# Head norms sent through DRAM, prepared blocks copied apart, softmax scaled on ScalarE

## The chip, the cores and the metric

The kernel runs on one core of one Trainium2 chip. A core has five engines with a queue each: TensorE (PE in the profile; its weight loads are PEld), VectorE (DVE), ScalarE (ACT), GpSimd (POOL) and SyncE (SP). ScalarE and SyncE also issue DMAs; an instruction that waits at the head of a queue holds everything behind it. The metric is the device time of one execution in microseconds. The kernel before takes 897.43 us (median of three runs, 896.43 to 899.38).

## The reference

One encoder layer in fp32 over 512 tokens (two sequences of 256, d_model 1024), with three branches on the same normalised input, each gated and projected, summed and projected once more:

```python
proj = rmsnorm(x) @ w_in                      # 1024 -> 9952 columns
# A: gated delta rule, 8 heads of 128, both directions, chunks of 64
o_gdn = rmsnorm(o_fwd + o_bwd, gdn_norm_gain) * silu(z_gdn)
# B: low-rank attention with rotary keys, 8 heads
p = softmax(q_full @ k_full.T * scale);  o_mla = (p @ v_mla) * silu(z_mla)
# C: cross attention into 256 memory tokens, 4 heads
o_mem = (softmax(qx @ km.T * scale) @ vm) * silu(z_mem)
merged = g0 * (o_gdn @ w_br_gdn) + g1 * (o_mla @ w_br_mla) + g2 * (o_mem @ w_br_mem)
y = rmsnorm(x + merged @ w_out)
```

The norm of branch A is one number for each token and head: the root of the mean square over the head's 128 channels.

## The kernel before

All activations are kept with channels on the partitions and the 512 tokens along the row. Every product is done in three passes of rounded fp32 (high times high, low times high, high times low). A weight tile of 512 KB is therefore loaded by SP, rounded to its high part by ScalarE (`wh_`, line 205) and subtracted to its low part by VectorE or, for the qkv, qn and qm tiles, GpSimd (`wl_`, line 209). Each of the three has two buffers. One tile gives 24 products of 512 columns (`gemm`, line 237).

The work has three stages. `front` does the memory branch and the low-rank attention (branch B), with projection tiles from the list `fill` put between. `attend` does one softmax: scores on TensorE, the maximum on VectorE, the exponential with its sum on ScalarE (`p_a`, line 301), the reciprocal of the sum (line 304) and the scaling (line 306) on VectorE, and then transpositions on TensorE (`pt_a`). `middle` does the gated delta rule: `weave` runs several chains (preparation of two groups of four heads, loads, inputs, two solving lanes, outputs) against an estimated clock `self.now`, and each `yield` gives the time that TensorE spends and the time to wait; while no chain is due, it takes tiles from `fill`. The order on TensorE is that of the writing there; the other engines are ordered by a scheduler, in which a chain's number (1000 for the preparation, 300 for inputs, 2000 for lanes and outputs) is its rank. `back` does the last branch product and the output.

What the change touches in `middle`: `gdn_prep` inverts small triangular blocks on VectorE (lines 821 and 823, 31 rounds) and then copies them with seven activations into `t32` and `y32` (lines 843 to 848). `gdn_out` sums the squares of a head's output over the partitions (`so`, line 1086), raises them to -1/2 on GpSimd (`ro`, line 1089), copies each of the 512 numbers to all 128 partitions with four products against the unit matrix (`rob`, line 273), and multiplies the head's output `og` by them (line 1094), which VectorE reads from PSUM. Then `og` is split into the two rounded parts `xg` that the branch product of `back` (`gm_bg`) reads.

`mem_v` starts the kernel. Its first activation (line 215) brings a load of ScalarE's function table.

Of the kernel before, what the change touches and what calls it, by code (L numbers as in the profile page):

```python
# [13 lines left out]
P = 128  # L14
# [26 lines left out]
def _consts():  # L41
    t = np.arange(P)
    b = t // 32
    same = b[:, None] == b[None, :]
    le = t[:, None] <= t[None, :]
    ge = t[:, None] >= t[None, :]
    z, o = np.zeros((P, P)), np.ones((P, P))
    a8 = np.arange(8)
    anc = np.zeros((P, 2, 2, 8))
    for tb in range(2):  # L50
        tg = tb * P + t
        anc[:, 0, tb] = tg[:, None] >= 32 * a8[None]
        anc[:, 1, tb] = tg[:, None] < 32 * (a8[None] + 1)
    i32 = np.arange(32)
    m = (t % 32)[:, None]
    parts = [
        ("id", np.eye(P)), ("bd", same),
        ("anc", anc.reshape(P, 32)),
        ("trf", m <= i32), ("trb", m >= i32), ("i32", m == i32),
        ("ngf", np.where(i32 > m, 0.0, NEG)), ("ngb", np.where(i32 < m, 0.0, NEG)),  # L60
        ("one", np.ones((P, 1))), ("hf", np.full((P, 64), -0.5)), ("ph", np.full((P, 16), 0.5)),
    ]
# [92 lines left out]
class Layer:  # L155
# [39 lines left out]
    def weight(self, src, n, name, pool=None):  # L195
# [13 lines left out]
        eng.tensor_tensor(lo[:, :n], raw[:, :n], hi[:, :n].bitcast(F32), op=ALU.subtract)  # L209
# [65 lines left out]


    def attend(self, h, s, score, scale, vs, op, name):
# [27 lines left out]
        for qb in range(2):  # L305
            nc.vector.tensor_scalar(pt[:, qb], pt[:, qb], rs[:, qb:qb + 1], None, ALU.mult)
# [423 lines left out]
    def gdn_prep(self, g):  # L730
# [109 lines left out]
        for a in range(4):  # L840
            r = slice(32 * a, 32 * a + 32)
            d = a % 2
            nc.scalar.activation(t32[r], (o2 if d else o1)[r, :, 16 * d:16 * d + 16].rearrange("p i u -> p u i"), AF.Copy)
            yield 0.0, 1.5
        nc.scalar.activation(y32[:, 0:16], o2[:, :, 0:16].rearrange("p i u -> p u i"), AF.Copy)
        yield 0.0, 2.5
        for q in range(2):
            nc.scalar.activation(y32[:, 16 + q:32:2], o1[:, :, 17 - q:32:2].rearrange("p i u -> p u i"), AF.Copy)
            yield 0.0, 1.5
        self.ready[g] = self.now + 10  # L850
# [202 lines left out]
    def gdn_out(self, hh):  # L1053
# [195 lines left out]
    def run(self):  # L1249
        nc = self.nc  # L1250
        with ExitStack() as st:
# [7 lines left out]
            self.d_xa = dp.tile([P, 8, 512], F32, name="d_xa")  # L1259
            self.d_m = dp.tile([8, P, 512], F32, name="d_m")  # L1260
# [19 lines left out]
    def plan(self):  # L1280
# [22 lines left out]
        self.fill += g[12:13] + z[4:5] + ze[2:3] + vt[6:7] + qv(7) + g[13:14] + z[5:6] + ze[3:4] + vt[7:8] + g[14:15] + xe  # L1303
        self.fill += z[6:7] + g[15:16] + z[7:8] + [(self.split_x, self.xe)]
# [68 lines left out]
    def middle(self):  # L1373
# [154 lines left out]
```

## Time and profile before

| | |
|---|---|
| median of three runs | 897.43 us (896.43 to 899.38) |
| profiled execution | 899.75 us, span 898.0 us, mean granted clock 0.993 |
| TensorE busy | 868.4 us (97%) |
| VectorE busy | 580.8 us (65%) |
| ScalarE busy | 458.0 us (51%) |
| GpSimd busy | 201.6 us (22%) |
| DMA | 114.03 MB, mean 127 GB/s |

Busy time on TensorE is time in which some product is under way; the granted clock is 1.00 at full speed. Idle time before an instruction is put down to what ended last before it. A shorter operation off TensorE changes the time only where TensorE waits for it.

### The profile page before, as it was taken

The numbers are of one execution on the slowest core, as the hardware profiler recorded it, in microseconds if no ns is written. First come the engines' busy times: TensorE is split into PE (matmuls) and PEld (weight loads), VectorE is DVE, ScalarE is ACT, GpSimd is POOL, SyncE is SP. The second block draws the span as 40 slices with busy tenths as digits, with TensorE's granted clock in tenths as the row PEclk, the third lists the DMA queues.
The fourth block names the chain that finished last, engine by engine and source line by source line (L and its number), as shares of the span: only waits on it lengthen the run. The fifth ranks groups of instructions, "written<-read, shape, count | busy, mean of one in ns | idle before, by whom it ended". The sixth has DMA issues, their size and how long they took to land.

```text
span 898.0 us, 13279 instructions
## 1 busy us (share of the span) xinstructions
PE 868.4 (97%) x4908; PEld 709.8 (79%) x4908; DVE 580.8 (65%) x993; ACT 458.0 (51%) x879; POOL 201.6 (22%) x149
## 2 busy tenths in 40 slices
PE   6999999999999989999999999999999999999996
PEld 5878886878888778877788877777888888888886
DVE  6685337876769999546689994757445444336643
ACT  6654455545544445466675658766563533213332
POOL 0230341121112210226133423422210001332221
PEclk9999999999999999999999999999999999999998
DMA  9312221442234322454323343444433436465332
GB/s 332 117 65 94 82 77 47 129 150 74 101 104 144 108 78 95 163 162 143 108 95 108 130 148 114 147 118 132 156 113 103 142 130 227 139 205 193 118 95 94
DMA packets 49313, 114.03 MB, mean 127 GB/s; under 512 B 6752, under 2 KB 12000, under 8 KB 49248
## 3 DMA queue, kind: packets, MB, share of 16 engines
q1 hardware_dynamic: 44496, 104.52, 35.6%
q10 hardware_dynamic: 4752, 8.65, 2.7%
q8 instruction: 39, 0.64, 0.3%
q14 instruction: 26, 0.21, 0.1%
HBM read 93.03 MB, written 16.97 MB: 123 GB/s over the span
## 4 chain that ended last, share of the span: by engine, by line
PE 79%; DVE 10%; ACT 4%; DMA 3%; issue 2%; POOL 1%; SPq 0%; ACTq 0%; POOLq 0%; DVEq 0%
PE gm_g L237 13%; PE gm_qkv L237 10%; PE gm_bm L237 5%; PE gm_z L237 5%; PE gm_bg L237 5%; PE y L1195 4%; PE gm_za L237 4%; PE vm L366 3%; PE gm_be L237 3%; PE gm_qm L237 3%; PE gm_km L237 3%; PE gm_cq L237 2%; PE s_a L287 2%; PE o L1070 2%; PE kk L920 2%
## 5 line engine op out<-in xcount | busy, mean ns | idle before, releaser
L209 POOL TENSOR_TENSOR wl_qkv<-wr_qkv,wh_qkv 128x1024 fp32r<-128x1024 f32 x24 | 59.8, 2493 | 138.5 <-ACT wh_qkv L205 53.3
L698 DVE SCALAR_TENSOR_TENSOR kq<-cz,prm,kq 128x510 f32<-128x510 f32 (+1 forms) x64 | 53.7, 838 | 20.6 <-ACT kq L691 20.1
L237 PE MATMUL gm_g<-hh,wh_g 128*128 128x512 f32 x192 | 53.7, 411 | 4.2 <-ACT cz L689 2.3
L209 DVE TENSOR_TENSOR wl_g<-wr_g,wh_g 128x1024 fp32r<-128x1024 f32 x24 | 29.8, 1242 | 38.5 <-ACT wh_g L205 15.0
L237 PE MATMUL gm_qkv<-hh,wh_qkv 128*128 128x512 f32 x192 | 51.7, 408 | 2.1 <-ACT gt_g L1129 1.2
L237 PE MATMUL gm_g<-hl,wh_g 128*128 128x512 f32 x192 | 52.0, 403 | 0.0
L237 PE MATMUL gm_g<-hh,wl_g 128*128 128x512 f32 x192 | 52.0, 401 | 0.0
L237 PE MATMUL gm_qkv<-hl,wh_qkv 128*128 128x512 f32 x192 | 51.9, 403 | 0.0
L237 PE MATMUL gm_qkv<-hh,wl_qkv 128*128 128x512 f32 x192 | 51.4, 400 | 0.0
L237 PEld LDWEIGHTS gm_g<-hh,wh_g 128*128 128x128 f32 x192 | 35.6, 192 | 13.0 <-ACT cz L689 3.2
L1165 POOL TENSOR_TENSOR mg<-mg,lg 128x512 f32<-128x512 f32 x16 | 28.2, 1760 | 74.5 <-DVE lg L1164 58.3
L237 PEld LDWEIGHTS gm_qkv<-hh,wh_qkv 128*128 128x128 f32 x192 | 35.8, 192 | 10.8 <-ACT gt_g L1129 1.6
L237 PEld LDWEIGHTS gm_qkv<-hl,wh_qkv 128*128 128x128 f32 x192 | 36.2, 191 | 8.7 <-issue 0.4
L237 PEld LDWEIGHTS gm_g<-hl,wh_g 128*128 128x128 f32 x192 | 36.0, 191 | 8.1
L237 PEld LDWEIGHTS gm_qkv<-hh,wl_qkv 128*128 128x128 f32 x192 | 35.2, 188 | 7.7
L237 PEld LDWEIGHTS gm_g<-hh,wl_g 128*128 128x128 f32 x192 | 35.2, 189 | 7.5
L1195 PE MATMUL y<-wh_wo,mh 128*128 128x512 f32 (+1 forms) x144 | 40.0, 370 | 0.0
L821 DVE TENSOR_TENSOR tm<-xx,tt 128x1 f32<-128x1 f32 (+30 forms) x62 | 38.5, 622 | 1.0
L205 ACT ACTIVATE wh_g<-wr_g 128x1024 fp32r<-128x1024 f32 x24 | 25.4, 1057 | 24.8 <-PE gm_g L237 10.8
L205 ACT ACTIVATE wh_qkv<-wr_qkv 128x1024 fp32r<-128x1024 f32 x24 | 25.4, 1057 | 24.3 <-DVE tm L821 5.2
L910 POOL TENSOR_TENSOR kl<-kq,kh 128x512 fp32r<-128x512 f32 x16 | 21.7, 1361 | 67.1 <-ACT kh L908 46.4
L237 PE MATMUL gm_bm<-xa,wh_bm 128*128 128x512 f32 x128 | 33.2, 399 | 0.0
(400 smaller groups left out, 2250.0 us busy)
## 6 DMA issues: line engine op xcount, KB each, us to landing
wr_qkv<-in_w_dram SPq DMA_DIRECT2D x24, 512.0 KB, 3.3
wr_g<-in_w_dram SPq DMA_DIRECT2D x24, 512.0 KB, 3.4
e<-d_r SPq DMA_DIRECT2D x64, 96.0 KB, 3.0
wr_z<-in_w_dram SPq DMA_DIRECT2D x12, 512.0 KB, 3.4
wr_za<-in_w_dram SPq DMA_DIRECT2D x8, 512.0 KB, 3.5
d_g<-gt_g ACTq DMA_DIRECT2D x16, 256.0 KB, 2.0
wr_bm<-in_w_dram SPq DMA_DIRECT2D x8, 512.0 KB, 3.3
lg<-d_g SPq DMA_DIRECT2D x16, 256.0 KB, 3.3
```

The source lines that it names most:

```text
L205: self.wround = nc.scalar.activation(hi[:, :n], raw[:, :n], AF.Copy).ins
L209: eng.tensor_tensor(lo[:, :n], raw[:, :n], hi[:, :n].bitcast(F32), op=ALU.subtract)
L237: nc.tensor.matmul(ps[:m], a[:, k * m:(k + 1) * m], xs[k][j], start=n == 0, stop=n == 3 * nk - 1)
L287: nc.tensor.matmul(sp[:, qb * 256:(qb + 1) * 256], a, b, start=j == 0, stop=j == n - 1)
L366: nc.tensor.matmul(vps[tb], ms[k][a][:, t], b[:, :512], start=k == 0 and i == 0, stop=k == 7 and i == 2)
L698: nc.vector.scalar_tensor_tensor(ys, zs, self.cw[:, f, m:m + 1], ys, ALU.mult, ALU.add)
L821: nc.vector.tensor_tensor(t3, xx[:, i:i + 1, 0:i].to_broadcast([P, i, i]), tt[:, 0:i, 0:i], op=ALU.mult)
L910: nc.gpsimd.tensor_tensor(lo, src, hi.bitcast(F32), op=ALU.subtract)
L920: nc.tensor.matmul(ps, a[:, k], b, start=i == 0, stop=i == 2)
L1070: nc.tensor.matmul(out, ub[:, d, s, cp], rhs, start=n == 0, stop=n == 3)
L1165: nc.gpsimd.tensor_tensor(self.merged[d], self.merged[d], gt, op=ALU.add)
L1195: nc.tensor.matmul(ps, xs[2 * j + q][a][:, t], b[:, q * 512 + c0:q * 512 + c1], start=j == 0 and n == 0, stop=j == 3 and n == 5)
```

## The change

Five things are edited. The head norms: `store_cols` transposes the column of norms to rows on VectorE and stores it in DRAM with four small DMAs on SP's queue; a chain of its own, `heads_norm`, comes at least 10 us later by the estimated clock, loads the row back to all partitions with one DMA on ScalarE's queue (`load_row`, behind the last weight rounding written so far), waits 6 us more, and multiplies and splits `og` in `gdn_norm`. The seven copies of the preparation each stand behind the last weight rounding, with longer steps between them, and the preparation's rank falls from 1000 to 100. The scaling of the softmax in branch B moves to ScalarE. A one-column activation is put at the start. Two small things: a constant is narrower, and the loads of `xe` stand one tile later in `fill`.

```diff
@@ weight
-        eng.tensor_tensor(lo[:, :n], raw[:, :n], hi[:, :n].bitcast(F32), op=ALU.subtract)
+        d = eng.tensor_tensor(lo[:, :n], raw[:, :n], hi[:, :n].bitcast(F32), op=ALU.subtract)
+        if eng is nc.vector:
+            self.wsplit = d.ins
@@ new
+    def store_cols(self, r, i):
+        nc = self.nc
+        nc.vector.transpose(out=self.rt, in_=r)
+        for b in range(4):
+            nc.sync.dma_start(self.d_n[i].rearrange("(j b i) -> b j i", j=4, b=4)[b], self.rt[32 * b:32 * b + 4])
+    def load_row(self, dst, i):
+        with self.tc.issue_after(self.wround):
+            self.nc.scalar.dma_start(dst, self.d_n[i:i + 1].to_broadcast([P, 512]))
@@ attend
-            nc.vector.tensor_scalar(pt[:, qb], pt[:, qb], rs[:, qb:qb + 1], None, ALU.mult)
+            if name[0] == "a":
+                nc.scalar.activation(pt[:, qb], pt[:, qb], AF.Copy, scale=rs[:, qb:qb + 1])
+            else:
+                nc.vector.tensor_scalar(pt[:, qb], pt[:, qb], rs[:, qb:qb + 1], None, ALU.mult)
@@ mem_v
+        warm = self.p0.tile([P, 1], F32, name="warm")
+        nc.vector.memset(warm, 0.0)
+        nc.scalar.activation(warm, warm, AF.Square)
@@ gdn_prep (the three kinds of copies alike)
-            nc.scalar.activation(t32[r], (o2 if d else o1)[r, ...].rearrange("p i u -> p u i"), AF.Copy)
-            yield 0.0, 1.5
+            with self.tc.issue_after(self.wround):
+                nc.scalar.activation(t32[r], (o2 if d else o1)[r, ...].rearrange("p i u -> p u i"), AF.Copy)
+            yield 0.0, 2.8
...
-        self.ready[g] = self.now + 10
+        self.ready[g] = self.now + 4
@@ gdn_out
-        rr = self.p0.tile([P, 4], F32, tag="c4", bufs=4, name=f"ro{hh}")
+        rr = self.rr[:, 0:4]
         nc.vector.tensor_scalar(rr, ssp[:, 0:4], 1.0 / 128, 128 * EPS * EPS, ALU.mult, ALU.add)
         nc.gpsimd.tensor_tensor(rr, rr, c("hf")[:, 0:4], op=ALU.pow)
-        yield 0.9, 7.0
-        bp = self.ps_ms(par, f"rob{hh}")
-        self.bcast(rr, bp)
+        self.store_cols(self.rr, hh)
+        self.og[hh] = og, self.now + 10.0
         yield 0.9, 0.0
-        nc.vector.tensor_tensor(og, og, bp, op=ALU.mult)
+
+    def gdn_norm(self, hh):
+        nc = self.nc
+        og = self.og[hh][0]
+        rb = self.tb(f"rob{hh}")
+        self.load_row(rb, hh)
+        yield 0.0, 6.0
+        with self.tc.issue_after(self.wsplit):
+            nc.vector.tensor_tensor(og, og, rb, op=ALU.mult)
         hl = self.pk.tile([P, 2, 512], F32R, tag="kq", bufs=8, name=f"xg{hh}")
         self.split(og, hl[:, 0], hl[:, 1], 0.5)
@@ plan, middle
-  ... + g[14:15] + xe + z[6:7] + g[15:16] + ...
+  ... + g[14:15] + z[6:7] + xe + g[15:16] + ...
-            self.weave((self.preps(), 1000), ..., (self.heads_out(), 2000))
+            self.weave((self.preps(), 100), ..., (self.heads_out(), 2000), (self.heads_norm(), 1500))
+    def heads_norm(self):
+        for h in range(8):
+            while h not in self.og or self.now < self.og[h][1]:
+                yield 0.0, 1.0
+            yield from self.gdn_norm(h)
```

The first place is ScalarE's queue in the attention stage, at one softmax of head 6 (`p_a61`), before the change (`wh_` is a weight's rounding, `gt_` a gate, `ph_` the rounded softmax):

```order
L301 ACTIVATE p_a61_3524,sm_a61_3525<-s_a61_3509,nb_a61_3522,rq_891 128x256 x2
L205 ACTIVATE wh_qkv12_3747<-wr_qkv12_3745 128x1024
L1129 ACTIVATE gt_g05_3589<-gm_g05_3564 128x512
L1135 DMA d_g_67<-gt_g05_3589 128x512
L215 ACTIVATE ph_a61_3537<-pt_a61_3532 128x512
L301 ACTIVATE p_a70_3642,sm_a70_3643<-s_a70_3627,nb_a70_3640,rq_891 128x256 x2
```

The same place in the changed kernel:

```order
L315 ACTIVATE p_a61_3528,sm_a61_3529<-s_a61_3513,nb_a61_3526,rq_895 128x256 x2
L321 ACTIVATE p_a61_3528<-p_a61_3528,rs_a61_3532 128x256 x2
L205 ACTIVATE wh_qkv12_3754<-wr_qkv12_3752 128x1024
L217 ACTIVATE ph_a61_3541<-pt_a61_3536 128x512
L1161 ACTIVATE gt_g05_3593<-gm_g05_3568 128x512
L1167 DMA d_g_68<-gt_g05_3593 128x512
L315 ACTIVATE p_a70_3646,sm_a70_3647<-s_a70_3631,nb_a70_3644,rq_895 128x256 x2
```

The two scalings now stand between the exponentials and the next weight's rounding, and the softmax's rounding has moved ahead of the gate.

The second place is ScalarE's queue where the attention stage ends and the first group's prepared blocks are copied (`t320` and `y320`), before the change:

```order
L205 ACTIVATE wh_g07_3926<-wr_g07_3924 128x1024
L843 ACTIVATE t320_3728<-o10_3710 32x512
L843 ACTIVATE t320_3728<-o20_3712 32x512
...
L845 ACTIVATE y320_3729<-o20_3712 128x512
L848 ACTIVATE y320_3729<-o10_3710 128x8x32 x2
L908 ACTIVATE kh00_3904<-kq0_1252 128x512
L908 ACTIVATE kh01_3908<-kq0_1252 128x512
L699 ACTIVATE cz_12_3808<-kq4_3807 128x512
L1129 ACTIVATE gt_g06_3851<-gm_g06_3823 128x512
```

The same place in the changed kernel:

```order
L205 ACTIVATE wh_g07_3933<-wr_g07_3931 128x1024
L719 ACTIVATE cz_12_3814<-kq4_3813 128x512
L1161 ACTIVATE gt_g06_3856<-gm_g06_3829 128x512
L1167 DMA d_g_68<-gt_g06_3856 128x512
L932 ACTIVATE kh00_3910<-kq0_1256 128x512
L932 ACTIVATE kh01_3914<-kq0_1256 128x512
L864 ACTIVATE t320_3735<-o10_3714 32x512
L864 ACTIVATE t320_3735<-o20_3716 32x512
...
L868 ACTIVATE y320_3736<-o20_3716 128x512
L872 ACTIVATE y320_3736<-o10_3714 128x8x32 x2
L205 ACTIVATE wh_qkv14_3967<-wr_qkv14_3965 128x1024
```

The block of copies is still in one piece; the gate's activation `gt_g06` and the two roundings `kh0` have moved ahead of it, and the rounding of the next weight, `wh_qkv14`, follows it.

The third place is SP's queue where the first head's norms are stored, before the change (`wr_` is a weight load, `vs4` the values of head 4):

```order
L200 DMA wr_z54_5216<-in_w8_dram 128x1024
L865 DMA vs4_5311<-d_v_60 64x512
L868 DMA vs4_5311<-d_v_60 64x2x128 x2
L200 DMA wr_qkv6_5340<-in_w8_dram 128x1024
L200 DMA wr_qkv22_5437<-in_w8_dram 128x1024
L1119 DMA zo_z54_5328<-d_om_62 128x512
```

The same place in the changed kernel:

```order
L200 DMA wr_z54_5222<-in_w8_dram 128x1024
L889 DMA vs4_5300<-d_v_60 64x512
L200 DMA wr_qkv6_5348<-in_w8_dram 128x1024
L892 DMA vs4_5300<-d_v_60 64x2x128 x2
L283 DMA d_n_66<-rt_3731 4x32 x4
L200 DMA wr_qkv22_5447<-in_w8_dram 128x1024
L200 DMA wr_g14_5511<-in_w8_dram 128x1024
L1153 DMA d_z_63<-zt_z31_5218 128x512
```

Four stores of norms have come in between two weight loads.

And ScalarE's queue where that row of norms is loaded back, in the changed kernel, where nothing stood before:

```order
L1167 DMA d_g_68<-gt_g13_5152 128x512
L985 ACTIVATE m0_3723<-na2_4679 64x2x64 x2
L288 DMA rob0_5197<-d_n_66 128x512
L205 ACTIVATE wh_qkv6_5350<-wr_qkv6_5348 128x1024
L719 ACTIVATE cz_21_5068<-vf5_5067 128x512
L1073 ACTIVATE ub1_4742<-us11_5205 64x2x128 x2
L1134 ACTIVATE zt_z31_5218<-gm_z31_5161 128x512
```

The load `rob0` stands directly ahead of the rounding of the qkv weight.

## Rows read from the trace of the kernel before

**Rows 1.** The page, part 1: busy time, share of the span, instructions.

```profile
PE 868.4 (97%) x4908; PEld 709.8 (79%) x4908; DVE 580.8 (65%) x993; ACT 458.0 (51%) x879; POOL 201.6 (22%) x149
```

**Rows 2.** Stretches: PE, PEld, DVE, ACT, POOL busy (instructions), clock, DMA share, GB/s.

```profile
0.00:25.00 25.00, 17.94 (x66) 14.34 (x67) 16.02 (x26) 15.60 (x27) 0.20 (x4) 1.00 0.92 335
...
300.00:325.00 25.00, 22.17 (x107) 17.53 (x105) 22.98 (x36) 11.41 (x21) 6.56 (x3) 1.00 0.33 111
325.00:350.00 25.00, 23.42 (x110) 19.19 (x110) 22.79 (x40) 9.54 (x20) 1.49 (x1) 0.93 0.22 76
...
400.00:425.00 25.00, 23.03 (x93) 18.22 (x92) 13.49 (x24) 16.55 (x30) 15.09 (x16) 0.93 0.57 174
...
500.00:525.00 25.00, 25.00 (x159) 20.82 (x159) 24.84 (x37) 16.50 (x35) 6.75 (x7) 1.00 0.35 116
525.00:550.00 25.00, 22.98 (x148) 18.78 (x147) 18.80 (x33) 18.25 (x30) 11.31 (x10) 1.00 0.38 118
550.00:575.00 25.00, 22.14 (x139) 17.57 (x138) 18.56 (x29) 16.84 (x40) 4.50 (x6) 1.00 0.54 169
...
875.00:900.00 25.00, 16.11 (x93) 13.90 (x91) 6.89 (x15) 6.08 (x14) 3.88 (x6) 0.86 0.22 85
```

**Rows 3.** Chain that ended last, 770 to 860: start us, us, what.

```profile
769.90 5.62 PE gm_bm L237 x24
775.52 0.89 PE rob L273 x8
776.41 24.83 PE gm_bm L237 x106
801.25 44.98 PE gm_bg L237 x192
```

**Rows 4.** Timeline from 0 to 26: start us, us, engine, operation.

```profile
4.99 1.28 ACT L215 ACT_TABLE_LOAD   x1 [4.99 <-DMA prm<-in_prm_dram]
...
7.06 3.78 PE L366 MATMUL vm<-wh_vm,mh 128*128 128x512 f32 x8 [7.06 <-ACT mh L215]
```

**Rows 5.** Timeline from 320 to 326.5, attention stage.

```profile
320.57 2.38 POOL L209 TENSOR_TENSOR wl_qkv<-wr_qkv,wh_qkv 128x1024 fp32r<-128x1024 f32 x1 [6.03 <-ACT wh_qkv L205]
...
320.88 2.49 DVE L306 TENSOR_SCALAR p_a<-p_a,rs_a 128x256 f32<-128x256 f32 x2
...
323.16 0.81 PE L310 MATMUL pt_a<-cst,p_a 128*128 128x128 f32 x4 [1.22 <-DVE p_a L306]
```

**Rows 6.** Line L306: count, ns min/median/max, first and last start.

```profile
L306 DVE TENSOR_SCALAR p_a<-p_a,rs_a x32: 340/349/2223, 200.5 to 383.5; 128x256 f32<-128x256 f32 x32
```

**Rows 7.** Groups on ScalarE by form: busy us, mean ns, idle before.

```profile
L301 ACT ACTIVATE p_a<-s_a,nb_a,rq 128x256 f32<-128x256 f32 x32 | 17.8, 560 | 16.5 <-DVE nb_a L296 16.5
...
L1029 ACT ACTIVATE u<-u 128x256 f32<-128x256 f32 x16 | 6.0, 378 | 5.6 <-PE u L1027 5.0 <-ACT gt_g L1129 0.4
```

**Rows 8.** Timeline from 395 to 405, where the stages change.

```profile
395.36 4.65 ACT L843 ACTIVATE t<-o 32x512 f32<-32x512 f32 x4
...
403.76 0.59 ACT L1129 ACTIVATE gt_g<-gm_g 128x512 f32<-128x512 f32 x1
...
404.40 1.14 PE L237 MATMUL gm_g<-hh,wh_g 128*128 128x512 f32 x3 [1.97 <-ACT gt_g L1129]
```

**Rows 9.** Waits of SP's queue: us in total, times, longest us.

```profile
SPq L200 <- POOL wl_qkv L209: 108.3, 20, 10.0
```

**Rows 10.** Instructions on tile ro: ns min/median/max.

```profile
L1088 DVE TENSOR_SCALAR ro<-so x8: 149/158/163, 512.2 to 768.4; 128x4 f32<-128x4 f32 x8
L1089 POOL TENSOR_TENSOR ro<-ro,cst x8: 1007/1009/1662, 512.5 to 768.8; 128x4 f32<-128x4 f32 x8
```

**Rows 11.** The page, part 6: KB each, median us from issue to landing.

```profile
e<-d_r SPq DMA_DIRECT2D x64, 96.0 KB, 3.0
...
d_g<-gt_g ACTq DMA_DIRECT2D x16, 256.0 KB, 2.0
```

**Rows 12.** Line L209, VectorE, branch weights: ns min/median/max.

```profile
L209 DVE TENSOR_TENSOR wl_bg<-wr_bg,wh_bg x8: 1217/2347/2353, 796.3 to 835.9; 128x1024 fp32r<-128x1024 f32 x8
```

More of the change, by code (lines that the diff above doesn't have):

```diff
@@ L60, in _consts @@
         ("ngf", np.where(i32 > m, 0.0, NEG)), ("ngb", np.where(i32 < m, 0.0, NEG)),
-        ("one", np.ones((P, 1))), ("hf", np.full((P, 64), -0.5)), ("ph", np.full((P, 16), 0.5)),
+        ("one", np.ones((P, 1))), ("hf", np.full((P, 4), -0.5)), ("ph", np.full((P, 16), 0.5)),
     ]
@@ L842, in gdn_prep @@
             d = a % 2
-            nc.scalar.activation(t32[r], (o2 if d else o1)[r, :, 16 * d:16 * d + 16].rearrange("p i u -> p u i"), AF.Copy)
-            yield 0.0, 1.5
-        nc.scalar.activation(y32[:, 0:16], o2[:, :, 0:16].rearrange("p i u -> p u i"), AF.Copy)
-        yield 0.0, 2.5
+            with self.tc.issue_after(self.wround):
+                nc.scalar.activation(t32[r], (o2 if d else o1)[r, :, 16 * d:16 * d + 16].rearrange("p i u -> p u i"),
+                                     AF.Copy)
+            yield 0.0, 2.8
+        with self.tc.issue_after(self.wround):
+            nc.scalar.activation(y32[:, 0:16], o2[:, :, 0:16].rearrange("p i u -> p u i"), AF.Copy)
+        yield 0.0, 2.8
         for q in range(2):
-            nc.scalar.activation(y32[:, 16 + q:32:2], o1[:, :, 17 - q:32:2].rearrange("p i u -> p u i"), AF.Copy)
-            yield 0.0, 1.5
-        self.ready[g] = self.now + 10
+            with self.tc.issue_after(self.wround):
+                nc.scalar.activation(y32[:, 16 + q:32:2], o1[:, :, 17 - q:32:2].rearrange("p i u -> p u i"), AF.Copy)
+            yield 0.0, 2.8
+        self.ready[g] = self.now + 4
         return t32, y32, cc
@@ L1259, in run @@
             self.d_xa = dp.tile([P, 8, 512], F32, name="d_xa")
+            self.d_n = dp.tile([8, 512], F32, name="d_n")
             self.d_m = dp.tile([8, P, 512], F32, name="d_m")
@@ L1302, in plan @@
         self.fill += qv(4) + g[10:11] + z[2:3] + ze[0:1] + vt[4:5] + qv(5) + g[11:12] + z[3:4] + ze[1:2] + vt[5:6] + qv(6)
-        self.fill += g[12:13] + z[4:5] + ze[2:3] + vt[6:7] + qv(7) + g[13:14] + z[5:6] + ze[3:4] + vt[7:8] + g[14:15] + xe
-        self.fill += z[6:7] + g[15:16] + z[7:8] + [(self.split_x, self.xe)]
+        self.fill += g[12:13] + z[4:5] + ze[2:3] + vt[6:7] + qv(7) + g[13:14] + z[5:6] + ze[3:4] + vt[7:8] + g[14:15]
+        self.fill += z[6:7] + xe + g[15:16] + z[7:8] + [(self.split_x, self.xe)]
         self.fill += xa + be
@@ L1385, in middle @@
         self.loads, self.loaded, self.started = {}, {}, set()
+        self.og = {}
+        self.rr, self.rt = (self.p0.tile([P, 32], F32, name=n) for n in ("rr", "rt"))
+        nc.gpsimd.memset(self.rr, 0.0)
         self.hd, self.ub, self.out, self.idle = {}, {}, 0, 0.0
@@ L1388, in middle @@
         with self.tc.manual_schedule(engines={mybir.EngineType.PE}):
-            self.weave((self.preps(), 1000), (self.heads_load(), 300), (self.heads_in(), 300), (self.lane(0), 2000), (self.lane(1), 2000),
-                       (self.heads_out(), 2000))
+            self.weave((self.preps(), 100), (self.heads_load(), 300), (self.heads_in(), 300), (self.lane(0), 2000), (self.lane(1), 2000),
+                       (self.heads_out(), 2000), (self.heads_norm(), 1500))
     def preps(self):
```

## The prediction

> **What bounds the kernel now.** I read the page's busy shares first, then the table of 25 us stretches, then the chain of waits, and only then single rows. TensorE is busy for 868.4 of 898.0 us [rows 1], so it is the bound nearly everywhere, and the questions are what leaves TensorE's own work and what leaves its idle time. The idle time is 29.5 us: 7.06 before the first product and 6.89 in the last, incomplete stretch, which leaves about 15.6 in the middle [rows 2]. It is not spread evenly: 2.83 + 1.58 us lie in 300 to 350, 1.97 in 400 to 425, 2.02 + 2.86 in 525 to 575 [rows 2]. In two of these stretches the granted clock averages 0.93: the lower level (1.2 instead of 2.4 GHz) for about 25 x 0.14 = 3.5 us, which costs 1.75 us of work each. Both follow a gap in TensorE's work. VectorE is nearly full in 300 to 350 and wholly full in 500 to 525 (24.84 of 25), while ScalarE has half its time left there [rows 2]. So the attention stage is where VectorE can hold TensorE up, the change from stage to stage at 400 is ScalarE's, and 525 to 575 follows VectorE's fullest stretch.
>
> **The change part by part**, against the profiled execution (899.75 us, of which the span is 898.0). That execution lies 2.3 us above the median of 897.43, and I take the differences over to the median.
>
> 1. The broadcast products of the head norms go: 8 heads, 4 products each, in the chain 0.89 us a head [rows 3]. TensorE's next work stands ready behind them, so all of it is gained: 8 x 0.89 = -7.1. Bounds: -7.1, and 0 if TensorE only meets its next wait that much earlier; I take the row, since the waits are few.
> 2. The dummy activation pulls the table load, 1.28 us, ahead of the first input. Today it starts at 4.99 when that input lands, and TensorE waits for the rounding behind it until 7.06 [rows 4]. Before 4.99 ScalarE only issues one DMA. -1.3; bounds 0 and -1.3, since nothing else of the start moves.
> 3. Softmax scaling leaves VectorE. 32 operations of 349 ns median, 2223 at the longest [rows 6]. The pair at 320.88 took 2.49 us instead of 0.70 because it ended only when GpSimd's 2.38 us subtraction from 320.57 had ended, and TensorE waited 1.22 us for that pair [rows 5]. That wait goes. The gaps of 300 to 350 sum to 4.4 and the clock after them cost 1.75, so the bound is -6.2. ScalarE gets 32 operations more: its nearest rows are 378 ns (a copy of 256 columns) and 560 (an exponential of 256 with two column operands) [rows 7], 12 to 18 us in a stage in which it is half idle. It now also waits for VectorE's reciprocal with the next weight's rounding queued behind; the order shows that. Were each of 16 halves late by twice the difference to VectorE, 16 x 2 x (0.56 - 0.35) = +6.7 is the other bound. Nearest is the row with TensorE's wait of 1.22 plus the clock that it cost; I take -3.0.
> 4. Copies of the preparation, group 0: they start at 395.36, four of the seven alone take 4.65 us, a gate's activation queued behind them starts at 403.76, and TensorE waits 1.97 us until 404.40 [rows 8]; with the clock 3.7 in all. In the changed order the seven copies still form one block, but that activation stands ahead of it, and a weight's rounding behind it. TensorE then has the product of the rounding before the block, 5.62 us [rows 3], against the 8.4 us that lie today between the block's start and that activation, so something of a gap may stay. -2.5; bounds -3.7 and +1.
> 5. The preparation of group 1 gets a lower rank than the heads, and its copies are held behind a weight's rounding. The gaps of 525 to 575, 4.9 us [rows 2], could all go, or, where the heads of group 1 become ready later, grow by as much. VectorE loses nothing else there. I take -1.5.
> 6. The new way of the norms: a 32-column transposition, four stores on SP's queue and one broadcast load on ScalarE's for each head. No row shows this transposition; VectorE's operation on the same norms takes 0.16 [rows 10], and at that size it is hidden. It waits for GpSimd's power, 1.0 to 1.7 us [rows 10], however, and stands directly behind the sum's scaling in the order of most heads, so VectorE stands still for over a microsecond each. Where VectorE has room that costs nothing; for the two heads that fall into its full stretch I charge something. The load waits for the stores; a store lands 2.0 us after issue and the nearest broadcast load takes 3.0 [rows 11]. Behind the load stands a rounding. Together +1.5; bounds 0 (a wait can't help TensorE) and +8 for two heads, each behind a GpSimd operation of 2.4 [rows 5] and a power of 1.7.
>
> The last head needs all this by 801.25, when the branch products begin with it as last operand; its broadcast is at 775.52 today and 24.83 us of other products follow [rows 3]. Power, issue, 2.0, 3.0 and the two roundings add some 10 us; hidden. The narrower constant and the order of xe loads cost nothing that a row prices: I set them to 0.
>
> Sum: -7.1 - 1.3 - 3.0 - 2.5 - 1.5 + 1.5 = -13.9. That makes 885.9 for the profiled execution and 883.5 for the median; I forecast 884.
>
> On step 3, rows give 349 ns on VectorE against 378 to 560 on ScalarE. The Trainium skill, "ScalarE: Activation LUTs" (Rules for kernel authors), advises VectorE for multiplications, and its section "What ACT_TABLE_LOAD costs" gives 186 + 0.833 ns an element and 93 for a column operand: an estimate of 492 ns here. By it the bound of +6.7 would be 16 x 2 x (0.492 - 0.349) = +4.6, and the forecast would lose its -3.0 too: 897.4 - 13.9 + 3.0 + 4.6 = 891. This is the third rival below, there by rows alone.
>
> On step 6, a subtraction of two SBUF tiles on VectorE took 2347 ns as a median, against 1217 at best, in the branch products' stage, where GpSimd's merging additions run beside it [rows 12]. "GPSIMD Engine Reference" (Specifications) of the Trainium skill says the two contend when VectorE has two SBUF inputs, which agrees; and the product of output and norm had one operand in PSUM and has none now. By it those eight products could take up to 1.1 us more, and for the two heads in the full stretch the sum would be 886 instead of 884.
>
> **The rivals.**
> - Only what is certain: the idle time in the middle moves but does not shrink, and steps 1 and 2 remain: 897.4 - 8.4 = 889. For it: the copies still form a block, and VectorE stays full at 500. Against: the wait in rows 5 has a cause that the change takes away.
> - More: the gaps of 300 to 350, of 404 and of 525 to 575 all go with their clock: -7.1 - 1.3 - 6.2 - 3.7 - 4.9 = -23.2, that is 874. For it: each has one named cause. Against: earlier TensorE work meets other waits.
> - ScalarE holds the attention stage: steps 1, 2, 4 to 6 hold, step 3 is +6.7: 897.4 - 13.9 + 3.0 + 6.7 = 893. For it: the reciprocal sits in VectorE's queue at 22.98 of 25 busy. Against: ScalarE is busy for 11.4 and 9.5 of 25 us there.
> - Slower: the stores stand on SP's queue among weight loads, which wait up to 10.0 us there for their buffer [rows 9]; ScalarE's load waits for the stores' landing at the head of its queue with the next rounding behind it. A store 10.0 late and landed 2.0 later holds ScalarE 12.0, TensorE has one product of 5.6 in hand, so up to 6.4 is lost; at half of that for each head it is 8 x 3.2 = +26 on the forecast without step 6's charge: 897.4 - 15.4 + 26 = 908. It decides from 18 us in all, 2.3 a head, a hold of about 8 us. For it: the order has a weight load just before the first stores and a rounding directly behind the load. Against: the load is placed 10 us after the stores.
> - That the change doesn't do what it says can be in step 4 alone, where the copies stay in one block; that is in its bounds.
>
> **How the numbers follow.** Forecast (879 to 888) 0.55; only the certain 0.17; more 0.12; ScalarE holds 0.07; slower 0.09. The forecast's own range is 879 to 888. The range for 8 in 10 is 875 to 895: it leaves out about half of "more", the slower case and a little of the third. About 0.3%, 2.7 us, is what a measurement can tell from no change. Faster by over that, below 894.7: the forecast, "more", nearly all of "only the certain" and most of the third, 0.83. Within: the rest of these two and a light form of the slower case, 0.08. Slower 0.09.
>
> **What would show it.** Step 1: no broadcast rows of the norms, TensorE busy near 861. Step 2: first product near 5.8, table load near 1.2. Step 3: no wait of the transposed scores for VectorE, the granted clock at 1.00 in 300 to 350, scaling rows on ScalarE between 378 and 560. Step 4: the gap at 404 under 1 us. Step 5: idle of 525 to 575 under 4. Step 6: ScalarE's idle time before the broadcast load under 2 us a head, VectorE's wait for the power near 1. The forecast is wrong if TensorE's idle time in the middle is above its 15.6 of now: then ScalarE's load or the weights behind the stores will be named before the products.

## The result and the profile after

| | before | changed |
|---|---|---|
| median, us | 898.09 (896.43 to 899.38, 4 runs) | 884.20 (884.01 to 886.43, 4 runs) |
| profiled execution, us | 899.75 | 884.01 |
| its span, us | 898.0 | 882.1 |

The ratio is 0.9852, 95% interval 0.9828 to 0.9876: 13.9 us less between the medians. The forecast was 884 (875 to 895).

The page of the changed kernel, part 1 (busy us, share of the span, instructions of each engine):

```profile
PE 859.3 (97%) x4844; PEld 703.2 (80%) x4844; DVE 571.2 (65%) x970; ACT 472.0 (54%) x912; POOL 201.9 (23%) x150
```

Against [rows 1], TensorE is busy for 9.1 us less, with 64 products fewer, and its idle time fell from 29.6 to 22.8 us. So a little over half of the 15.9 us of span is work, and the rest is waiting. Where the waiting went, the stretches of 25 us show (PE, PEld, DVE, ACT, POOL busy, then granted clock, DMA share, GB/s):

```profile
0.00:25.00 25.00, 19.30 (x74) 15.56 (x75) 17.27 (x29) 17.10 (x31) 0.33 (x5) 1.00 0.93 338
...
300.00:325.00 25.00, 22.57 (x104) 17.99 (x103) 24.73 (x39) 11.48 (x25) 6.01 (x3) 0.93 0.32 106
325.00:350.00 25.00, 24.42 (x116) 19.71 (x116) 21.82 (x33) 11.72 (x25) 1.02 (x1) 0.93 0.20 67
400.00:425.00 25.00, 25.00 (x139) 20.11 (x138) 16.18 (x28) 20.63 (x42) 14.04 (x16) 1.00 0.57 169
500.00:525.00 25.00, 25.00 (x130) 21.21 (x130) 23.82 (x33) 15.80 (x33) 8.24 (x5) 1.00 0.42 131
525.00:550.00 25.00, 22.92 (x165) 17.91 (x164) 15.88 (x32) 24.32 (x46) 7.46 (x8) 0.93 0.52 152
550.00:575.00 25.00, 23.71 (x148) 19.48 (x146) 17.25 (x34) 15.98 (x35) 10.30 (x9) 1.00 0.42 140
```

Read beside [rows 2]: the start gives 1.36, 300 to 350 only 1.40 (idle 4.41 to 3.01), 400 to 425 all its 1.97, 525 to 575 1.51 (4.88 to 3.37). The granted clock averages 0.93 in three stretches instead of two. At the prediction's price of 1.75 us for each, that is one price more: 300 to 350 now pays two instead of one, 400 none, 525 to 550 a new one. So the first surprise is that 300 to 350, for which the scaling was moved, gained only 1.4 us of idle time, while 404 is wholly clean.

A second profile of the very same kernel (the run called "the reference again" below) tells what of this is steady:

```profile
300.00:325.00 25.00, 22.56 (x109) 17.93 (x108) 24.72 (x40) 11.35 (x25) 5.27 (x3) 1.00 0.31 106
325.00:350.00 25.00, 24.42 (x127) 20.10 (x126) 23.77 (x33) 15.02 (x28) 1.02 (x1) 1.00 0.20 67
525.00:550.00 25.00, 23.07 (x171) 18.44 (x170) 15.92 (x31) 23.72 (x48) 5.21 (x8) 1.00 0.46 149
550.00:575.00 25.00, 21.42 (x135) 17.86 (x134) 14.29 (x29) 16.10 (x38) 12.39 (x11) 0.95 0.41 134
```

The idle time of 300 to 350 is the same (3.02 us), the start gives 1.29 and 400 to 425 again all its 1.97. But the clock is 1.00 in 300 to 350, and 525 to 575 idles for 5.51 us, more than before the change. So the gain of 525 to 575 and the clock of single stretches differ between executions of one kernel and can't be put down to the edit.

Three waits of TensorE that are left (timeline; in brackets the idle time before and who ended it):

```profile
319.87 0.51 PE L301 MATMUL s_a<-kn,qnh 128*128 128x256 f32 x2 [0.72 <-ACT qnh L217]
322.39 3.78 PE L239 MATMUL gm_qkv<-hh,wh_qkv 128*128 128x512 f32 x8 [1.64 <-DVE za L1135]
...
535.58 1.05 PE L1110 MATMUL so<-cst,sq 128*128 128x1 f32 x8 [1.96 <-DVE sq L1106]
```

The wait for the scaled scores in [rows 5] is gone, but a product a little later waits longer for VectorE's gate (`za`). In the kernel before, that wait was 0.90 us, and the one ahead of it 0.45:

```profile
304.14 2.15 PE L237 MATMUL gm_qkv<-hh,wh_qkv 128*128 128x512 f32 x8 [1.16 <-ACT gt_g L1129]
...
324.66 0.39 PE L319 MATMUL oa<-ph_a,vh 128*128 128x256 f32 x1 [0.45 <-ACT ph_a L215]
325.94 3.32 PE L237 MATMUL gm_qkv<-hh,wh_qkv 128*128 128x512 f32 x8 [0.90 <-DVE za L1103]
```

So the waits around the scaled pair fell only from 2.57 us (1.22 + 0.45 + 0.90) to 2.36 (0.72 + 1.64). Most of what 300 to 350 gained is the wait at 304 for a gate's activation on ScalarE (`gt_g`), which the changed kernel doesn't have.

The start, from the timeline: the table load and the first product, to be read beside [rows 4].

```profile
1.18 1.28 ACT L354 ACT_TABLE_LOAD   x1 [1.18 <-PEq L1559]
...
5.70 0.80 PE L386 MATMUL vm<-wh_vm,mh 128*128 128x512 f32 x1 [5.70 <-ACT mh L217]
```

The scaling's line (count, ns min/median/max, first and last start), which answers to [rows 6]:

```profile
L321 ACT ACTIVATE p_a<-p_a,rs_a x32: 492/500/523, 198.6 to 383.3; 128x256 f32<-128x256 f32 x32
```

The norms' tile after the sum: the power, the transposition, and in the last line what VectorE waited for (us in total, times).

```profile
L1113 POOL TENSOR_TENSOR rr<-rr,cst x8: 1007/1012/1437, 508.2 to 754.2; 128x4 f32<-128x4 f32 x8
L281 DVE STREAM_TRANSPOSE rt<-rr x8: 202/211/213, 510.9 to 755.2; 128x32 f32<-128x32 f32 x8
...
  POOL rr L1113: 5.9, 5
```

The same for the tile that the broadcast load fills, with the product that takes it:

```profile
L288 ACTq DMA_DIRECT2D rob<-d_n x8: 326/326/327, 513.7 to 758.2; - x8
L1126 DVE TENSOR_TENSOR og<-og,rob x8: 682/692/1881, 519.0 to 765.0; 128x512 f32<-128x512 f32 x8
...
  DMA rob<-d_n: 7.7, 3
```

VectorE stood 5.9 us for the power and 7.7 for the broadcast load (in the kernel before, 6.0 for the broadcast products), and the largest waits of TensorE after 500 are for the squares (`sq`), a decay product (`p1s`, 1.37) and `w` (1.12), never for the norms.

### The profile page after: what moved, and what is told of

The parts are those of the page before. It is cut to its first block, busy times and chain, and to the rows that moved or that the text cites. A ratio compares the mean times of both kernels' runs of the same rounds, so it can differ in the third digit from the quotient of the medians.

```text
span 882.1 us, 13248 instructions
## 1 busy us (share of the span) xinstructions
PE 859.3 (97%) x4844; PEld 703.2 (80%) x4844; DVE 571.2 (65%) x970; ACT 472.0 (54%) x912; POOL 201.9 (23%) x150
## 4 chain that ended last, share of the span: by engine, by line
PE 85%; DVE 7%; ACT 3%; DMA 2%; issue 1%; POOL 1%; SPq 0%; POOLq 0%; DVEq 0%; ACTq 0%
PE gm_g L239 14%; PE gm_qkv L239 13%; PE gm_z L239 6%; PE gm_bg L239 5%; PE gm_bm L239 5%; PE y L1227 4%; PE gm_za L239 4%; PE vm L386 3%; PE gm_qm L239 3%; PE gm_km L239 3%; PE gm_be L239 2%; PE kk L944 2%; PE gm_cq L239 2%; PE s_a L301 2%; PE o L1094 2%
## 5 line engine op out<-in xcount | busy, mean ns | idle before, releaser
L209 POOL TENSOR_TENSOR wl_qkv<-wr_qkv,wh_qkv 128x1024 fp32r<-128x1024 f32 x24 | 60.7, 2531 | 141.2 <-ACT wh_qkv L205 35.9
L239 PE MATMUL gm_g<-hh,wh_g 128*128 128x512 f32 x192 | 51.3, 400 | 1.0 <-ACT cz L709 1.0
L209 DVE TENSOR_TENSOR wl_g<-wr_g,wh_g 128x1024 fp32r<-128x1024 f32 x24 | 30.5, 1271 | 26.4 <-ACT wh_g L205 9.6
```

The source lines that it names most:

```text
L209: d = eng.tensor_tensor(lo[:, :n], raw[:, :n], hi[:, :n].bitcast(F32), op=ALU.subtract)
L239: nc.tensor.matmul(ps[:m], a[:, k * m:(k + 1) * m], xs[k][j], start=n == 0, stop=n == 3 * nk - 1)
```

## The experiments

The twelve runs came in three sets of four; each set was timed beside the kernel before on its own chip, so the ratios are the thing to compare. For the chips of the first set (scaling, norms, copies with rank, and dummy activation undone) and of the last, no run of the changed kernel is on record. "Worth" is what the part that a run undoes, or the edit that it adds, takes off the time: the ratio's distance from the changed kernel's 0.985 (for the two built on the kernel before, from 1), times 897 us.

| run | median, us | ratio to before, 95% | worth, us |
|---|---|---|---|
| changed, first runs | 884.20 | 0.9852 (0.9828 to 0.9876) | |
| changed again | 883.95 | 0.9841 (0.9828 to 0.9854) | |
| qkv passes on VectorE: no effect, the changed kernel a third time | 886.26 | 0.9861 (0.9840 to 0.9882) | |
| scaling back on VectorE | 886.23 | 0.9892 (0.9873 to 0.9910) | 3.8 |
| norms by products again | 889.61 | 0.9934 (0.9914 to 0.9954) | 7.5 |
| copies and rank as before | 891.70 | 0.9947 (0.9931 to 0.9963) | 8.7 |
| rank alone as before | 884.55 | 0.9855 (0.9837 to 0.9872) | 0.4 |
| copies alone as before | 891.04 | 0.9929 (0.9914 to 0.9945) | 7.1 |
| no dummy activation | 887.90 | 0.9910 (0.9889 to 0.9930) | 5.4 |
| before + scaling on ScalarE | 892.58 | 0.9968 (0.9952 to 0.9985) | 2.9 |
| before + tied copies | 897.96 | 1.0013 (0.9994 to 1.0033) | -1.2 |
| changed + gate first | 883.47 | 0.9853 (0.9829 to 0.9878) | -0.3 |
| changed + one pass on VectorE | 885.65 | 0.9874 (0.9843 to 0.9904) | -2.2 |

Three measurements of one and the same kernel span 0.9841 to 0.9861: differences under about 2 us say nothing by their medians, and there only the profile speaks.

**The reference again.** No edit.

> The changed kernel itself, on the same chip as the others of this set, so that they have a reference: 884.2 if the first runs stand. If the four undo experiments are right as they are, that is 0.3 to 0.9% below each of them. If it comes out at 886 or more, a part of what they seemed to cost was the chip.

Measured 883.95, but on another chip than the first four undo runs; these are compared with it by their ratios alone, and so they stand.

**Norms by products again.**

```diff
-        self.store_cols(self.rr, hh)
-        self.og[hh] = og, self.now + 10.0
+        yield 0.9, 7.0
+        bp = self.ps_ms(par, f"rob{hh}")
+        self.bcast(rr, bp)
         yield 0.9, 0.0
...
+        nc.vector.tensor_tensor(og, og, bp, op=ALU.mult)
...
```

The chain `heads_norm` goes with it.

> The changed kernel with the head norms spread by broadcast products on TensorE again (no store, no broadcast load, no chain of its own). Theory A, step 1 with step 6 (-7.1 + 1.5): 889.8, TensorE busy 7 to 9 us more. Theory B, the detour costs nothing: 884.2 + 7.1 = 891.3. Theory C, TensorE only met its next wait earlier: under 886.5, with the idle time in the middle smaller by what the busy time grew.

5.4 us more by the medians, 7.5 by the ratios, between A and B. TensorE's busy time rose by 7.8:

```profile
PE 867.1 (97%) x4908; PEld 713.1 (80%) x4908; DVE 570.1 (64%) x962; ACT 472.7 (53%) x912; POOL 200.8 (23%) x150
```

C is out: TensorE's idle time is 23.3 us against 22.8, so the products add to its time. A and B, that is the detour's price between 0 and 1.5, can't be told apart.

**Scaling back on VectorE.**

```diff
-            if name[0] == "a":
-                nc.scalar.activation(pt[:, qb], pt[:, qb], AF.Copy, scale=rs[:, qb:qb + 1])
-            else:
-                nc.vector.tensor_scalar(pt[:, qb], pt[:, qb], rs[:, qb:qb + 1], None, ALU.mult)
+            nc.vector.tensor_scalar(pt[:, qb], pt[:, qb], rs[:, qb:qb + 1], None, ALU.mult)
```

> The changed kernel with the softmax scaling of the attention back on VectorE, all else as changed (884.2). Theory A, the prediction's step 3 (-3.0): without it 887.2, and TensorE waits for the scaled scores by VectorE again, one pair near 2.2 us. Theory B, read from the trace after: the gap only moved (idle time of 300 to 350 went from 4.41 to 3.00 us, but the stretch at the lower clock from 3.41 to 6.83 us), so the step was worth about 0.3 us gain or less: 884.2 plus or minus 1. Theory C, the 32 operations of 500 ns on ScalarE cost more than they free: below 883.

2.0 us by the medians, 3.8 by the ratios: about A in size. But its profile has three waits again, and the largest is at the change of stages, for which the prediction had named the copies. This kernel's copies are tied as in the changed one:

```profile
301.61 2.13 PE L239 MATMUL gm_qkv<-hh,wh_qkv 128*128 128x512 f32 x8 [1.33 <-ACT gt_g L1158]
...
320.63 0.81 PE L324 MATMUL pt_a<-cst,p_a 128*128 128x128 f32 x4 [1.27 <-DVE p_a L320]
...
400.06 2.12 PE L239 MATMUL gm_g<-hh,wh_g 128*128 128x512 f32 x8 [1.96 <-ACT gt_g L1158]
```

**Before, with only the scaling moved.** The same lines, the other way round, in the kernel before.

> The kernel before with only the softmax scaling of the attention moved to ScalarE. Theory A, the prediction's step 3 alone: the wait of 1.22 us for the scaled scores goes and 1.75 us of clock with it, 897.4 - 3.0 = 894.4, the gap at 404 still there, since its cure was to be step 4. Theory B, from the undo runs (the gap at 404 came back when only the scaling was undone and stayed away when only the copies were): the gap at 404 goes with this edit alone, 1.97 + 1.75 = 3.7, while 300 to 350 keeps about its idle time: 893.7. Both give nearly the same time; the gap at 404 in the profile tells them apart. Theory C: ScalarE holds the attention, 897.4 or more.

2.9 us less: both theories' size, and each is right in part. With the copies not tied, TensorE is busy for 24.99 of 25 us from 400, as B says; and the wait for the scaled scores is gone, as A says, with the idle time of 300 to 350 down from 4.41 to 2.96 us, which B had not. On ScalarE the gate's activation now stands ahead of the block of copies:

```profile
393.29 0.60 ACT L1132 ACTIVATE gt_g<-gm_g 128x512 f32<-128x512 f32 x1
...
394.30 4.66 ACT L846 ACTIVATE t<-o 32x512 f32<-32x512 f32 x4 [0.40 <-ACT gt_g L1132]
```

**Before, with only the copies tied** (the seven copies, their pauses and their ready time).

```diff
-            nc.scalar.activation(t32[r], (o2 if d else o1)[r, :, 16 * d:16 * d + 16].rearrange("p i u -> p u i"), AF.Copy)
-            yield 0.0, 1.5
+            with self.tc.issue_after(self.wround):
+                nc.scalar.activation(t32[r], (o2 if d else o1)[r, :, 16 * d:16 * d + 16].rearrange("p i u -> p u i"),
+                                     AF.Copy)
+            yield 0.0, 2.8
...
-        self.ready[g] = self.now + 10
+        self.ready[g] = self.now + 4
```

> The kernel before with only the preparation's copies tied to a weight's rounding (their pauses and ready time too). Theory A, the prediction's step 4 alone (-2.5): 894.9, the gap at 404 under 1 us. Theory B, the undo run (+7.1 when only the copies are as before) gives the edit's worth wherever it stands: 890. Theory C, the copies became costly only through the other parts, which moved group 1's copies beside the heads' products: here -2 at most from the small gaps of 525 to 575, 895.5, and the gap at 404 stays.

No gain, and A and B are out. The copies form one block as before, the gate's activation stands behind it, and TensorE waits; ScalarE first, then TensorE, both from the timeline.

```profile
395.43 4.61 ACT L844 ACTIVATE t<-o 32x512 f32<-32x512 f32 x4
...
403.80 0.57 ACT L1133 ACTIVATE gt_g<-gm_g 128x512 f32<-128x512 f32 x1
```
```profile
404.43 0.73 PE L237 MATMUL gm_g<-hh,wh_g 128*128 128x512 f32 x2 [1.92 <-ACT gt_g L1133]
```

C's first half (the gap at 404 stays) holds. Its -2 at most didn't come either: 525 to 550 has one gap of 3.56 us in place of several small ones.

**Copies and rank as before**, and then each alone (the lines above reversed; the rank is the number beside `preps`, 100 against 1000).

> The changed kernel with the preparation as before: the copies not tied to a weight's rounding, their old pauses, and the higher rank over the heads. Theory A, steps 4 and 5 (-2.5 and -1.5): 888.2. Theory B, by the trace after: the gap at 404 comes back with its clock (1.97 + 1.75 = 3.7) while 525 to 575 changes by nothing, its smaller gaps having been paid by a new stretch at the lower clock: 887.9, with the clock at 1.00 in 525 to 550. Theory C, gaps only move: 884.2 plus or minus 1.

> The changed kernel with only the preparation's rank as before (over the heads); its copies stay tied to the weight's rounding. Theory A, the prediction's step 5 (-1.5): 885.7, the gap at 404 still gone. Theory B, from the run with both parts undone (891.7, twice the forecast 4): the rank carries most of it, 888 to 890, with waits of TensorE over 2 us between 520 and 545. Theory C, the rank changes nothing: 884.2.

> The changed kernel with only the preparation's copies as before (not tied to a rounding, old pauses and ready time); the lower rank stays. Theory A, the prediction's step 4 (-2.5): 886.7 with the gap at 404 back at near 2 us. Theory B, the copies carry most of the 7 us: 889 or more. Theory C, they change nothing, since the gap at 404 was closed by another part: 884.2 and no gap at 404.

Both: 7.5 us by the medians, more than A and B allowed, and no gap at 404. The rank alone: 0.4, theory C. The copies alone: 6.8 and 7.1, the second theory, and without the gap at 404 that step 4 lays to the copies. A part of what they cost lies at group 1. The untied copies fill ScalarE without a break from 529.07 to 536.13; a gate's activation stands behind them and behind 2.4 us of other work, and TensorE waits for its product (rows of the kernel with only the copies as before):

```profile
532.69 2.32 ACT L863 ACTIVATE t<-o 32x512 f32<-32x512 f32 x2
...
535.01 1.12 ACT L865 ACTIVATE y<-o 128x512 f32<-128x512 f32 x1
...
538.41 0.59 ACT L1130 ACTIVATE zt_z<-gm_z 128x512 f32<-128x512 f32 x1
...
539.04 0.69 DVE L1131 SCALAR_TENSOR_TENSOR zt_z<-zt_z,gm_z 128x512 f32<-128x512 f32 x1 [1.04 <-ACT zt_z L1130]
...
539.78 1.31 PE L239 MATMUL gm_qkv<-hh,wh_qkv 128*128 128x512 f32 x3 [2.82 <-DVE zt_z L1131]
```

In the changed kernel the tie opens the block, and the same activation runs between two copies:

```profile
529.68 0.67 ACT L872 ACTIVATE y<-o 128x256 f32<-128x256 f32 x1
530.25 0.58 ACT L1134 ACTIVATE zt_z<-gm_z 128x512 f32<-128x512 f32 x1
530.86 2.34 ACT L864 ACTIVATE t<-o 32x512 f32<-32x512 f32 x2
```

With the copies as before TensorE also waits 2.64 for a product of the decay at 527, 1.07 at 705, 1.64 at 740 and 1.40 at 742, where the changed kernel's first profile has 1.96, 1.37 and 1.12 in all; its clock averages 0.86 in 525 to 550 and in 725 to 750. Against the second profile of the changed kernel (5.51 us idle in 525 to 575, here 5.19) the gap at group 1 is no loss. The steady difference is in 700 to 750: 4.15 us idle here and 4.90 with the rank undone too, against 1.13 to 1.74 in three profiles of the changed kernel. What brings the waits there was not tested.

**No dummy activation.**

```diff
-        warm = self.p0.tile([P, 1], F32, name="warm")
-        nc.vector.memset(warm, 0.0)
-        nc.scalar.activation(warm, warm, AF.Square)
```

> The changed kernel without the dummy activation at the start. Theory A, step 2 (-1.3): 885.5, table load near 5 us, first product near 7.06. Theory B, the earlier start only moves what TensorE meets next: 884.2.

3.7 us by the medians, 5.4 by the ratios, more than the 1.42 by which the first product is late (7.12 against 5.70). This run's profile has two gaps that the changed kernel's first profile lacks, 0.68 at 303.51 and 0.83 at 749.54 (its third has one of 0.58 there, too), and its six times spread from 885.34 to 890.13. A's row is there; the rest stays open.

**The qkv passes on VectorE.**

```diff
-        eng = nc.gpsimd if name[0] == "q" or name == "km3" else nc.vector
+        eng = nc.gpsimd if (name[0] == "q" and name != "qkv") or name == "km3" else nc.vector
```

> The changed kernel with the subtraction of the qkv weights (2.56 us on GpSimd) on VectorE, so that no GpSimd pass runs beside VectorE's two-input operations in 300 to 350. Theory A, the pass is what holds VectorE there (a 0.74 us operation took 2.07 beside it, and TensorE then waits 1.64 us for the gate): that operation falls to 0.74, the gap at 322 under 0.5, the clock is 1.00 in 325 to 350: 880 to 882. Theory B, VectorE is simply full there and gets 1.2 us more for each weight: the gap stays or grows, 884 to 888.

The names carry numbers (`qkv19`), so no weight met the condition; the pass is still on GpSimd in this profile, and it tells nothing of either theory. The edit was made again for one weight:

```diff
-        eng = nc.gpsimd if name[0] == "q" or name == "km3" else nc.vector
+        eng = nc.gpsimd if (name[0] == "q" and name != "qkv19") or name == "km3" else nc.vector
...
-        if eng is nc.vector:
+        if eng is nc.vector and name != "qkv19":
```

> The changed kernel with one subtraction of a weight (qkv19, 2.56 us on GpSimd from 317.31) on VectorE; all others as they are. Theory A, GpSimd's pass is what makes the 0.69 us operation of VectorE beside it take 2.07: here it takes 0.7. The gap at 322 then depends on the scores that VectorE's next operation waits for (they end at 320.37) and stays at 1.5 to 1.7, the time at 884. Theory B, the pass has nothing to do with it: the operation still takes about 2 us. Theory C, the contention sets the gap: it falls by over 1 us, 880 to 882.

A in its first half. The operation that took 2.07 us beside GpSimd's pass takes 0.68 without it, and the wait at 322 is still 1.39. A's reason for that, a maximum that waits for scores, isn't seen here: VectorE works without a break up to the gate's product, now with the moved pass (1.22 us) in its queue. So the run gives VectorE back nearly what it took away, and doesn't tell what the contention by itself costs TensorE:

```profile
318.10 0.68 DVE L720 SCALAR_TENSOR_TENSOR kq<-cz,kq 128x512 f32<-128x512 f32 x1
318.70 1.22 DVE L209 TENSOR_TENSOR wl_qkv<-wr_qkv,wh_qkv 128x1024 fp32r<-128x1024 f32 x1
...
321.89 2.50 PE L239 MATMUL gm_qkv<-hh,wh_qkv 128*128 128x512 f32 x5 [1.39 <-DVE za L1135]
```

What no theory had: one pass on another engine brought the gap at the change of stages back, 2.06 us at 399.55, because in this order the gate's activation fell behind the copies once more, though they are tied and the scaling is on ScalarE:

```profile
392.15 4.70 ACT L864 ACTIVATE t<-o 32x512 f32<-32x512 f32 x4
...
398.92 0.57 ACT L1161 ACTIVATE gt_g<-gm_g 128x512 f32<-128x512 f32 x1
```

**Gate first.** An attempt at a better kernel: the recursion's last steps and one maximum stand behind the gate's product in VectorE's order.

```diff
-        nc.vector.tensor_reduce(mx, s3, axis=AX.X, op=ALU.max)
+        with self.tc.issue_after(self.zh) if name == "a41" else nullcontext():
+            nc.vector.tensor_reduce(mx, s3, axis=AX.X, op=ALU.max)
...
-            nc.vector.tensor_tensor(
-                t3, xx[:, i:i + 1, 0:i].to_broadcast([P, i, i]), tt[:, 0:i, 0:i], op=ALU.mult)
+            with self.tc.issue_after(self.zstt) if g == 0 and i >= 25 else nullcontext():
+                nc.vector.tensor_tensor(
+                    t3, xx[:, i:i + 1, 0:i].to_broadcast([P, i, i]), tt[:, 0:i, 0:i], op=ALU.mult)
```

`zstt` is the latest gate's product on VectorE, `zh` that of the head at hand.

> The changed kernel with two ties on VectorE: the last seven steps of the preparation's recursion of group 0 stand behind the next gate, and in head 4 the maximum of the second scores stands behind the gate's product, so that the gate no longer waits behind a maximum whose scores come late (0.68 us) and a recursion step (0.80). Theory A: the gap of 1.64 us at 322 falls to 0.4 or less, and the stretch at the lower clock behind it goes: 884 - 1.3 - 3.4 = 879 to 881. Theory B, the gap goes but the clock stays, since it follows the gap of 0.72 before it too: 882 to 883. Theory C, the recursion's end and with it the first copies come too late for the heads: 885 or more, with a wait near 400.

883.47, no difference that can be told. The gaps of 0.72 and 1.64 became one of 1.93, which now rests on the operation beside GpSimd's pass (2.08 us). The timeline shows it:

```profile
317.34 2.08 DVE L721 SCALAR_TENSOR_TENSOR kq<-cz,kq 128x512 f32<-128x512 f32 x1
319.34 0.67 DVE L1137 SCALAR_TENSOR_TENSOR za<-za,gm_za 128x512 f32<-128x512 f32 x1
320.07 3.61 PE L239 MATMUL gm_qkv<-hh,wh_qkv 128*128 128x512 f32 x8 [1.93 <-DVE za L1137]
```

The idle time of 300 to 350 fell from 3.01 to 2.00 us. Of the two stretches of 25 us only the first averages a clock of 0.93 here, which, by the two profiles of the changed kernel, one execution can't lay to the edit:

```profile
300.00:325.00 25.00, 23.00 (x106) 18.53 (x105) 22.11 (x36) 11.83 (x26) 5.00 (x3) 0.93 0.30 106
325.00:350.00 25.00, 25.00 (x139) 21.49 (x138) 17.95 (x28) 14.57 (x29) 1.04 (x1) 1.00 0.24 84
```

So none of the theories: the gap's cause went from the one in VectorE's order to the one that the run with one pass on VectorE took away. Both edits in one kernel were not tried.

## Why the prediction was right, and where it was not

The time was right, in part by luck. Steps 1 and 2 held. Step 3 had its size by a mechanism that was half another, step 4 cured nothing where it was placed and was worth more elsewhere, and steps 5 and 6 were near nothing.

1. The norms' products, -7.1: right. In the kernel before, some product of the norms is under way for 8.4 us (64 records of 275 ns, which overlap), somewhat more than the chain's 8 x 0.89, and the undo run found 5.4 to 7.5 for them together with the detour.
2. The dummy activation, -1.3: the start agrees (1.36). The undo run cost more, for which there is no settled cause.
3. The scaling, -3.0: the size is right (2.9 alone, 2.0 to 3.8 undone), the mechanism only in part. The step said that the wait for the scaled pair goes and the clock with it. The wait went, and the next in line took most of its place: VectorE remained the bound of 300 to 325 (24.73 of 25 busy, more than before), so the gate was late instead. "What is late next" was asked of the copies and not here. The gain came from two other waits, both for a gate's activation on ScalarE. The one at 304 is 1.10 to 1.33 us in the three kernels with the scaling on VectorE and absent with it on ScalarE, but for 0.68 in the run without the dummy activation; the idle time of 300 to 350 is 4.18 to 4.62 us in the former and 2.96 to 3.02 in the eight profiles of the latter that change nothing else up to there. Why that wait goes was not tested. The one at 404 goes by a changed order of ScalarE, and three runs show that: it goes in the kernel before with this edit alone, comes back with this edit undone, and stays away with only the copies undone. The clock is no part of it: one and the same kernel has 0.93 in both stretches of 300 to 350 in one profile and 1.00 in another.
4. The copies, -2.5 by the gap at 404: wrong. In the kernel before, the tie gave nothing and left the gap as it was. With the other parts in place it is worth 7, for which the step charged nothing: not at 404, but, by the idle time, above all in 700 to 750. The error was to take one instance of a cure (the gate ahead of the block) for the doing of the edit that stood nearest to it in the order. Whether the gate's activation stands ahead of the block decides: with it ahead no gap over 0.2 us (the changed kernel, scaling alone, copies alone as before, and all the others), with it behind 1.92 to 2.06 us (before, copies alone, scaling undone, one pass moved), whatever the tie.
5. The rank, -1.5: nothing that can be measured (0.4). The gaps of 525 to 575 are 3.37, 5.51 and 3.62 us in three profiles of the changed kernel and 4.88 before; with the old rank they are 1.64 + 1.86, within that.
6. The detour, +1.5: not seen. VectorE waited 13.6 us for power and load, and TensorE for neither directly. ScalarE was held behind the load once, for 2.9 us.

Undone one by one, the parts are worth 25.4 us by the ratios (3.8 + 7.5 + 8.7 + 5.4, the copies and the rank counted once) and 18.6 by the medians; together they gave 13.9. They aren't a sum: the tie was worth nothing in the kernel before and 7 us in the changed one. Which of the other parts makes the untied copies costly was not tested.

What the profiles show as gone in all three of the changed kernel is 7.1 to 8.4 us of products, 1.3 to 1.4 at the start, 1.4 in 300 to 350 and 2.0 at 404: some 12 to 13 of the 13.9 us.

Of the rivals, ScalarE doesn't hold the attention: the scaling takes 500 ns, and TensorE waited for it once, 0.3 us. The Trainium skill, "ScalarE: Activation LUTs" (What ACT_TABLE_LOAD costs), gives 186 + 0.833 ns an element and 93 for a column operand, an estimate of 492 ns; the trace agrees within 2%. The stores behind weight loads were never late enough for TensorE to wait for them.

VectorE slowed down twice beside GpSimd: the same operation takes 0.68 us alone and 2.07 beside GpSimd's pass, and the product with the norms 0.69 as a median and 1.88 at its longest. "GPSIMD Engine Reference" (Specifications) of the Trainium skill says that the two contend when VectorE has two SBUF inputs, which agrees. The slow product cost TensorE nothing, which was busy for all of 500 to 525. The other stood directly ahead of the gate in the gate-first kernel, where TensorE waited 1.93 us; what the contention costs by itself stays open.

## What to carry to other kernels

Where a scheduler orders the queues, an edit's gain can lie where the order changes, not where the edit stands; look in the order for which instruction that TensorE needs stands behind a long block, and ask the same of every variant. Test a part both ways, alone in the kernel before and undone in the kernel after: this one's ties were worth nothing in the one and 7 us in the other. When a wait on a full engine goes, ask for the same engine's next result: here 2.57 us of waits became 2.36. And take a second profile of the same kernel before laying a clock or a single gap to an edit.

## What the runs showed of the hardware

The granted clock after a gap was not the same from one execution to the next. The changed kernel has gaps of 0.72 and 1.64 us at 322 in its first profile, and the clock averages 0.93 in both stretches of 300 to 350, which is the lower level (1.2 instead of 2.4 GHz) for a seventh of the time; in its second profile gaps of 0.72 and 1.65 are followed by 1.00 in both. With the scaling alone put into the kernel before, gaps of 0.72 and 1.65 were followed by 1.00 too. And the clock goes with the time of one kernel from run to run: of the five runs of the set in which the edit had no effect, the two with a mean granted clock of 0.992 and 0.996 have spans of 880.7 and 880.0 us, the three with 0.989 to 0.990 spans of 884.2 to 885.1. That it is most of what limits the medians here is likely and not shown; what decides the clock after such a gap stays open.

The contention of VectorE with GpSimd could be taken away and put back: 2.07 us with the pass beside it, 0.68 without, for the same operation at the same place.
